# Convolution blocks copied out of their PSUM banks, state-space groups that begin one burst earlier, and two half products ahead of the last group's output

## The chip, the cores and the metric

The kernel runs on one core of a Trainium2 chip. The metric is the device time of the core in microseconds (us), the lower the better. The kernel before takes 2576.32 us, the median of 3 runs (2575.54 to 2577.38).

## The reference

Two layers of a decoder trunk on 512 tokens of width 1024, everything in fp32. Each layer is a SwiGLU feed-forward half-step, a mixer and a second half-step:

```
x <- x + 1/2 * SwiGLU_1(RMSNorm(x))
h  = RMSNorm(x)
[q|k|v|z|xBC|dt|g_sb|g_ssm] = h @ W_in
y_sb  = StickBreakingAttention(q,k,v) @ W_branch_sb     (4 heads x 128)
y_ssm = Mamba2_SSD(z,xBC,dt) @ W_branch_ssm             (24 heads x 64, 8 B/C groups, state 128)
x <- x + (sigmoid(g_sb)*y_sb + sigmoid(g_ssm)*y_ssm) @ W_out
x <- x + 1/2 * SwiGLU_2(RMSNorm(x))
```

`Mamba2_SSD` first sends the xBC columns through a causal depthwise convolution of 4 taps and a SiLU, then runs a scan over four chunks of 128 tokens for each of 8 groups of 3 heads:

```
xbc = silu(causal_depthwise_conv(xbc, conv_w, conv_b)); xs, bm, cm = split(xbc)
cb = C_k B_k^T;  decay = exp(cum_t - cum_s) where s <= t
y_intra = (cb * decay) @ (x * dt);  y_inter = (C @ state) * exp(cum)
new_state = state * exp(cum_end) + (B * to_end)^T @ (x * dt)
y = (y + D * x) * silu(z);  y = y / rms of its group (192 wide) * ssm_norm
```

## The kernel before, in words

**Products.** Every large product is taken in fp32 by three passes of TensorE: weights and activations are split in a high part (`hi`) and a rest (`lo`), and for each block of 128 along the contraction `dense` issues three matmuls at L359, L360 and L361. The weights come block by block through `wraw` (three buffers, DMA issued by SP at L274), are cast to `whi` on ScalarE (L324) and subtracted to `wlo` on VectorE (L326), two units ahead of their use. A unit is the weights of one product (8 blocks; the merge products with `w_branch_ssm` have 12 blocks in two units of 6).

**What sets the order.** The order of each engine's instructions is written out by the program itself: `dense` calls `tick()` after each block of three matmuls, and a tick moves all side tasks (generators set going by `spawn`) one step on; `yield n` waits n ticks. The engines run their rows in that order, each in its own queue, and wait for one another by semaphores. Small matmuls of the side tasks are collected into bursts that stand between two blocks (`gather` sets the tick of the next burst and how many PSUM banks of each pool it may take, `meet` waits for such a place).

**PSUM.** Dense products use four banks `mm`; two banks `pa` and two banks `pt` serve the side tasks. A `mm` bank is reused four products later, once everything that reads it has run.

**The mixer.** After q, k, v and attention, `group_steps` gives an order of projection blocks of 128 columns: b, c and x blocks go to `conv_block`, z blocks to `by_tokens`, which takes all four `mm` banks at once, one for each 128 tokens (384 columns of weights). A pair of groups p = 0 to 3 shares one z block (2 x 192 columns) and three x blocks. `conv_block` reads the product's bank four times: once on ScalarE for the tap without a shift and the bias (L1112), three times on VectorE for the shifted taps (L1115, result `cv` in SBUF). A tanh on ScalarE (L1120) and one more VectorE instruction (L1127) make the SiLU; x and b blocks are then transposed by TensorE (L939) and copied out (L1145, L1154).

**A state-space group** (`ssd_group`, 8 a layer). For each chunk, `prepare` computes `xw` and `xdt` on GpSimd (L1226, L1234), the decays `dec` on ScalarE (L1236, L1238) from cumulative sums `cumb` that SP loads with one buffer (L1190), a mask on GpSimd (L1240) and y = D*x on GpSimd (L1242). `inner` multiplies C by B and the states by TensorE (L1246, L1250), `decay` applies `dec` (L1260), `outer` takes two chunks together (L1268, L1271), adds them to y (L1275 to L1283), multiplies by z (L1287) and sums squares (L1294). When all four chunks are there, GpSimd makes the reciprocal root (L1334, L1335), VectorE and ScalarE apply it (L1343, L1345), TensorE transposes the result (L939) and `y_part` splits it into `yt` (L1364, L1366), the input of the merge products. The next group begins when `ssd_on` becomes False.

**The end of the mixer.** After the last projection come two products of the attention branch (`branch_sb`); `flush` then ticks until all side tasks are done, among them the last group's output; then the merge loop takes for each of 8 column blocks the product of the 12 `yt` blocks with `w_branch_ssm`, in two halves of 6, in the order 6, 7, 0, 1, ... 5. Line numbers move on by 6 at the products and by up to 24 in `ssd_group` with the change.

Of the kernel before, what the change touches and what calls it, by code (L numbers as in the profile page):

```python
# [17 lines left out]
P = 128  # L18
# [9 lines left out]
HPG = 3  # L28
# [26 lines left out]
FRONT = 2  # L55
MERGE_ORDER = tuple(range(EARLY, KB)) + tuple(range(EARLY))
# [67 lines left out]
def unit_order(layer):  # L124

    def ffn(f):
        for s, (j0, j1) in enumerate(slices(layer, f)):
            start = j0
            if s == 0 and not pairs_from(layer, f):
                for key in leading(layer, f):  # L130
                    yield key, KB
                j0 = 4
            for j in range(j0, j1):
                if j < pairs_from(layer, f):
                    yield (layer, f, "gate", j), KB
                    yield (layer, f, "up", j), KB
                elif j % 2 == 0:
                    for part in SEVEN:
                        yield (layer, f, "pair", j, part), KB
            for m in OUT_ORDER:  # L140
                yield (layer, f, "down", s, m), j1 - start

    yield from ffn(1)
    for key in leading(layer, 0):
        yield key, KB
    for t, h in qkv_order():
        yield (layer, t, h), KB
    for kind, i in group_steps():
        if kind == "z":
            for u in range(NT):  # L150
                yield (layer, "z", i, u), 2 * 2 * GW // P + (i == 0)
        else:
            yield (layer, kind, i), KB
    for m in MERGE_ORDER[:2]:
        yield (layer, "bsb", m), SBH
    for i, m in enumerate(MERGE_ORDER):
        yield (layer, "bssm", m, 0), 6
        yield (layer, "bssm", m, 1), 6
        if i + 2 < KB:
            yield (layer, "bsb", MERGE_ORDER[i + 2]), SBH  # L160
    for m in OUT_ORDER:
        yield (layer, "out", m), KB
    yield from ffn(2)
# [12 lines left out]
class Builder:  # L176
# [63 lines left out]
    def meet(self, tag, limit):  # L240

        while self.burst != self.now or not self.free[tag]:
            if limit <= 0 and self.burst <= self.now:
                self.gather(1)
            limit -= 1
            yield 1
        self.free[tag] -= 1

# [855 lines left out]
    def conv_block(self, kind, i, ps):  # L1104
# [7 lines left out]
        nc.scalar.activation(u, ps, AF.Identity, scale=tap[KCONV - 1], bias=tap[KCONV])  # L1112
        yield 2
        for j in range(1, KCONV):
            nc.vector.scalar_tensor_tensor(u[:, j:], ps[:, :SEQ - j], tap[KCONV - 1 - j], u[:, j:],  # L1115
                                           op0=ALU.mult, op1=ALU.add)
            yield 1
# [14 lines left out]
        if kind == "x":  # L1132
            p, i = divmod(i, 3)
            yield from self.meet("pt", (10, 4 + 3 * (p == 0), 10)[i])
# [14 lines left out]
        elif kind == "b":  # L1149
            yield from self.meet("pt", 5)  # L1150
            pt = self.transposed(dst, NT - 1)
            yield 1
            tok = self.t(mp, [P, NT - 1, P], "btok")
            nc.scalar.copy(tok, pt)  # L1154
            self.ssm[i]["btok"] = tok
# [40 lines left out]
    def ssd_group(self, layer, g):  # L1196
# [10 lines left out]
        y = self.t(mp, [P, NT, GW], "y", bufs=1)  # L1207
        ss = self.t(mp, [P, NT], "ss")
        decs, xdts, xws, states, sums = {}, {}, {}, {}, {}
        finished = []  # L1210

        def heads(ap):
            return ap.rearrange("p (h d) -> p h d", d=HD)

        def wide(ap):
            return ap.unsqueeze(2).to_broadcast([P, HPG, HD])
# [11 lines left out]
        def prepare(c):  # L1228
# [13 lines left out]
            nc.gpsimd.tensor_tensor(heads(y[:, c, :]), x, wide(par[:, G_D + h0:G_D + h0 + HPG]), op=ALU.mult)  # L1242
# [19 lines left out]
        def outer(c0):  # L1262
# [10 lines left out]
            yield 2  # L1273
            yc = y[:, c0:c0 + 2, :]
# [28 lines left out]
        self.spawn(prepare(1), 3)  # L1303
        yield 5
# [13 lines left out]
        self.spawn(prepare(3), 5)  # L1318
        yield 8
# [4 lines left out]
        if g < GROUPS - 1:  # L1324
            self.spawn(self.next_cum(g + 1), 1)
        yield 2
        self.gather(1, 2, 0)
        self.spawn(outer(2))
        while len(finished) < NT:
            yield 1  # L1330
        self.give("xs")
        yield 1
        rstd = self.t(mp, [P, NT], "gny")
# [12 lines left out]
        self.ssd_on = False  # L1346
# [6 lines left out]
        for src, blk in todo:  # L1353
            yield from self.meet("pa", 8 if g < GROUPS - 1 else 0)
            pt = self.transposed(src.rearrange("p c d -> p (c d)"), aside=True).rearrange("p c d -> p (c d)")
            self.spawn(self.y_part(pt, blk, par[:, G_SSM + blk:G_SSM + blk + 1]))
# [44 lines left out]
    def mixer(self, layer):  # L1401
# [24 lines left out]
        with ExitStack() as mix:  # L1426
# [18 lines left out]
            with tc.tile_pool(name=f"mp{layer}", bufs=2, reuse_waits="tile") as self.mp:  # L1445
                self.attention_on, self.ssd_on, self.dt_done = False, False, False
                self.groups_left, self.cumb = GROUPS, None
# [25 lines left out]
                for m in MERGE_ORDER[:2]:  # L1473
                    branch_sb(m)
                self.flush()
            with tc.tile_pool(name=f"mg{layer}", bufs=KB, reuse_waits="tile") as mg, \
# [18 lines left out]
                for i, m in enumerate(MERGE_ORDER):  # L1495
                    ps = self.t(self.pmm, [P, SEQ], "mm")
                    self.dense(ps, self.unit(layer, "bssm", m, 0), self.y_ssm, 0, 6, stop=False)
                    self.dense(ps, self.unit(layer, "bssm", m, 1), self.y_ssm, 6, 12, start=False)
                    self.spawn(merge(i, ps))
                    if i + 2 < KB:  # L1500
                        branch_sb(MERGE_ORDER[i + 2])
# [174 lines left out]
```

## Time and profile before

| quantity | value |
|---|---|
| median of 3 runs | 2576.32 us (2575.54 to 2577.38) |
| profiled execution, its own time | 2577.66 us |
| its span in the trace | 2576.0 us, so 1.66 us lie around it |
| mean granted TensorE clock | 0.995 |
| TensorE busy in the span | 2545.2 us, so 30.8 us idle |
| VectorE, ScalarE, GpSimd busy | 1795.5, 1323.5, 551.5 us |

Both layers' state-space stages lie at 560 to 832 us and 1835 to 2108 us of the span. In the profile's rows a name such as `mm<-whi,hhi` reads as output from inputs, PE is TensorE, PEld its weight load, DVE VectorE, ACT ScalarE, POOL GpSimd, SP SyncE; a `q` behind an engine's name is its DMA queue. The clock is told as a share of full speed.

### The profile page before, as it was taken

To read this page: it belongs to the slowest core of one execution; us is meant where nothing else is said; L and a number is where in the kernel's file an instruction comes from. 1 tells how busy PE (TensorE), PEld (TensorE's weight loads), DVE (VectorE), ACT (ScalarE), POOL (GpSimd) and SP (SyncE) were. 2 spreads that over 40 slices of the span, in tenths; PEclk is the share of its full clock that TensorE was granted. 3 is DMA by queue.
4 is the path that set the end of the run, shared out by engine and by line. 5 is a ranking of instruction groups with operands and counts; after the bars stand their busy time and mean duration, and the time that the engine had idled before them with its cause. 6 is when DMAs were issued, how large, how long until landed. Compare 5 with 4: busy or idle time off the path is not lost.

```text
span 2576.0 us, 39402 instructions
## 1 busy us (share of the span) xinstructions
PE 2545.2 (99%) x15536; PEld 2301.7 (89%) x15536; DVE 1795.5 (70%) x2332; ACT 1323.5 (51%) x2181; POOL 551.5 (21%) x656
## 2 busy tenths in 40 slices
PE   9999999999999999999999999999999999999998
PEld 8899998888887889989899999988888878899997
DVE  8586886666765477768896768856666644885766
ACT  6353565665554264435563445656655533653434
POOL 0131300124433001313112222001344320122220
PEclk9999999999999999999999999999999999999999
DMA  4555673232222475656656466622333234756562
GB/s 152 168 140 159 170 203 112 78 114 100 91 91 86 140 209 148 179 152 164 180 126 179 144 174 175 194 80 82 115 99 101 93 94 159 193 140 169 151 164 83
DMA packets 112874, 357.35 MB, mean 139 GB/s; under 512 B 12784, under 2 KB 20400, under 8 KB 112688
## 3 DMA queue, kind: packets, MB, share of 16 engines
q1 hardware_dynamic: 96704, 299.13, 35.1%
q0 software_dynamic: 15120, 55.06, 11.9%
q8 instruction: 122, 2.00, 0.3%
q10 hardware_dynamic: 864, 0.64, 0.1%
q14 instruction: 64, 0.52, 0.1%
HBM read 342.10 MB, written 12.68 MB: 138 GB/s over the span
## 4 chain that ended last, share of the span: by engine, by line
PE 92%; DVE 4%; ACT 2%; issue 1%; POOL 1%; DMA 0%; DVEq 0%; SPq 0%; POOLq 0%; ACTq 0%
PE mm L359 25%; PE mm L361 25%; PE mm L360 25%; PE pa L360 4%; PE pa L359 4%; PE pa L361 4%; PE pa L1268 2%; DVE wlo L326 1%; DVE cv L1115 1%; PE pa L1271 1%; ACT whi L324 1%; PE pt L939 1%; PE pt L1250 1%; PE pt L1246 0%; PE pa L498 0%
## 5 line engine op out<-in xcount | busy, mean ns | idle before, releaser
L324 ACT CAST whi<-wraw 128x1024 fp32r<-128x1024 f32 (+3 forms) x433 | 427.8, 988 | 684.2 <-PE mm L361 436.4
L326 DVE TENSOR_TENSOR wlo<-wraw,whi 128x1024 fp32r<-128x1024 f32 (+3 forms) x433 | 532.7, 1230 | 246.7 <-ACT whi L324 246.0
L359 PE MATMUL mm<-hhi,whi 128*128 128x512 f32 (+1 forms) x1472 | 501.0, 340 | 0.3 <-DVE z L1184 0.3
L361 PE MATMUL mm<-hlo,whi 128*128 128x512 f32 (+1 forms) x1472 | 494.8, 336 | 0.0
L360 PE MATMUL mm<-hhi,wlo 128*128 128x512 f32 (+1 forms) x1472 | 494.3, 336 | 0.0
L361 PEld LDWEIGHTS mm<-hlo,whi 128*128 128x128 f32 x1472 | 276.0, 187 | 30.2
L359 PE MATMUL mm<-th,whi 128*128 128x256 f32 x1080 | 302.2, 280 | 0.8 <-DVE c L648 0.8
L360 PE MATMUL mm<-th,wlo 128*128 128x256 f32 x1080 | 301.6, 279 | 0.2 <-DVE wlo L326 0.2
L359 PEld LDWEIGHTS mm<-hhi,whi 128*128 128x128 f32 x1472 | 276.4, 188 | 28.1 <-DVE z L1184 1.0
L360 PEld LDWEIGHTS mm<-hhi,wlo 128*128 128x128 f32 x1472 | 276.6, 188 | 27.6
L361 PE MATMUL mm<-tl,whi 128*128 128x256 f32 x1080 | 301.3, 279 | 0.0
L326 DVE TENSOR_TENSOR wlo<-s,whi 128x1024 fp32r<-128x1024 f32 x180 | 257.2, 1441 | 35.3 <-ACT whi L324 31.7
L359 PE MATMUL mm<-act,whi 128*128 128x512 f32 (+1 forms) x710 | 273.9, 386 | 0.0
L360 PE MATMUL mm<-act,wlo 128*128 128x512 f32 (+1 forms) x710 | 273.7, 386 | 0.0
L361 PE MATMUL mm<-act,whi 128*128 128x512 f32 (+1 forms) x710 | 273.7, 385 | 0.0
L658 POOL TENSOR_TENSOR g<-g,rs 128x512 f32<-128x512 f32 x70 | 149.3, 2132 | 481.8 <-DVE g L637 452.2
L286 POOL DMA_DIRECT2D s<-in_wflat_dram x105 | 91.9, 900 | 726.4 <-DMA s<-in_wflat_dram 630.6
L324 ACT CAST whi<-s 128x1024 fp32r<-128x1024 f32 x180 | 188.7, 1048 | 61.4 <-PE mm L361 42.2
L359 PEld LDWEIGHTS mm<-th,whi 128*128 128x128 f32 x1080 | 202.7, 188 | 1.0 <-issue 1.0
L361 PEld LDWEIGHTS mm<-tl,whi 128*128 128x128 f32 x1080 | 202.9, 188 | 0.0
L360 PEld LDWEIGHTS mm<-th,wlo 128*128 128x128 f32 x1080 | 202.2, 187 | 0.4 <-DVE wlo L326 0.4
L721 DVE SCALAR_TENSOR_TENSOR x<-mm,x 128x512 f32<-128x512 f32 x93 | 64.2, 690 | 190.2 <-PE mm L361 190.0
(310 smaller groups left out, 5311.0 us busy)
## 6 DMA issues: line engine op xcount, KB each, us to landing
wraw<-in_wflat_dram SPq DMA_DIRECT2D x321, 512.0 KB, 3.6
s<-in_wflat_dram POOLq DMA_DIRECT2D x105, 512.0 KB, 7.5
s<-in_wflat_dram SPq DMA_DIRECT2D x95, 512.0 KB, 5.1
wraw<-in_wflat_dram SPq DMA_DIRECT2D x88, 384.0 KB, 3.1
cumb<-cum_d SPq DMA_DIRECT2D x16, 768.0 KB, 4.5
xd<-x SPq DMA_DIRECT2D x16, 256.0 KB, 5.5
wraw<-in_wflat_dram SPq DMA_DIRECT2D x16, 256.0 KB, 3.4
x<-xd SPq DMA_DIRECT2D x16, 256.0 KB, 5.2
```

The source lines that it names most:

```text
L286: self.nc.gpsimd.dma_start(raw, self.stored(key[:-1] + (part,)), accum_op=ALU.add)
L324: nc.scalar.copy(hi[:, :n], raw[:, :n])
L326: nc.vector.tensor_tensor(lo[:, :n], raw[:, :n], hi[:, :n].bitcast(F32), op=ALU.subtract)
L359: mm(ps, a[0], b[0], start=start, stop=False, **kw)
L360: mm(ps, a[1], b[0], start=False, stop=False, **kw)
L361: mm(ps, a[0], b[1], start=False, stop=stop, **kw)
L658: eng.tensor_tensor(out, r, self.rs[:, cols].unsqueeze(1).to_broadcast([P, 2, SEQ // 2]), op=ALU.mult)
L721: self.nc.vector.scalar_tensor_tensor(x, pd, 0.5, x, op0=ALU.mult, op1=ALU.add)
L939: self.nc.tensor.transpose(pt[:, cs], src[:, cs], self.ident)
L1115: nc.vector.scalar_tensor_tensor(u[:, j:], ps[:, :SEQ - j], tap[KCONV - 1 - j], u[:, j:], op0=ALU.mult, op1=ALU.add)
L1250: nc.tensor.matmul(pu, btok[:, c, :], xws[c].rearrange("p h d -> p (h d)"), start=True, stop=True)
L1268: nc.tensor.matmul(near[:, at:at + HD], decs[c][:, i, :], xdts[c][:, i, :], start=True, stop=True)
```

## The change

**Convolution.** ScalarE first copies the bank to the SBUF tile `raw` (which later takes the tanh); the activation and the three VectorE instructions then read that copy. A bank is free when the copy is done.

**State-space groups.** `ssd_on` becomes False one tick behind the second `outer` and no longer behind the normalisation. y = D*x moves out of `prepare` into a task `direct` of two chunks each, which takes the one y tile when the group before has normalised its own (`y_busy`); `outer` waits for it. The load of the next group's `cumb` is set going some ticks earlier. The transposes of y may use a `pa` or a `pt` bank and look for a place for up to 16 ticks, no longer 8.

**Merge.** With AHEAD = 2, the first halves of products 6 and 7 (blocks 0 to 5 of `yt`, 18 matmuls each) stand ahead of `flush`, so ahead of the last group's transposes; the order of the weight units follows.

```diff
+AHEAD = 2
@@ units
+    for m in MERGE_ORDER[:AHEAD]:
+        yield (layer, "bssm", m, 0), 6
     for i, m in enumerate(MERGE_ORDER):
-        yield (layer, "bssm", m, 0), 6
+        if i >= AHEAD:
+            yield (layer, "bssm", m, 0), 6
         yield (layer, "bssm", m, 1), 6
@@ Builder
-    def meet(self, tag, limit):
-
-        while self.burst != self.now or not self.free[tag]:
+    def meet(self, limit, *tags):
+
+        while self.burst != self.now or not any(self.free[tag] for tag in tags):
...
+        tag = next(tag for tag in tags if self.free[tag])
         self.free[tag] -= 1
+        return tag
@@ conv_block
-        nc.scalar.activation(u, ps, AF.Identity, scale=tap[KCONV - 1], bias=tap[KCONV])
+        nc.scalar.copy(r, ps)
+        nc.scalar.activation(u, r, AF.Identity, scale=tap[KCONV - 1], bias=tap[KCONV])
         yield 2
         for j in range(1, KCONV):
-            nc.vector.scalar_tensor_tensor(u[:, j:], ps[:, :SEQ - j], tap[KCONV - 1 - j], u[:, j:],
+            nc.vector.scalar_tensor_tensor(u[:, j:], r[:, :SEQ - j], tap[KCONV - 1 - j], u[:, j:],
@@ ssd_group
-        y = self.t(mp, [P, NT, GW], "y", bufs=1)
-            nc.gpsimd.tensor_tensor(heads(y[:, c, :]), x, wide(par[:, G_D + h0:G_D + h0 + HPG]), op=ALU.mult)
+        def direct(c0):
+            while self.y_busy not in (None, g):
+                yield 1
+            if self.y_busy is None:
+                self.y_busy = g
+                begun.append(self.t(mp, [P, NT, GW], "y", bufs=1))
+            for c in (c0, c0 + 1):
+                nc.gpsimd.tensor_tensor(heads(begun[0][:, c, :]), heads(xs[:, c, :]),
+                                        wide(par[:, G_D + h0:G_D + h0 + HPG]), op=ALU.mult)
+            begun.append(c0)
...
+            while c0 not in begun:
+                yield 1
...
         self.spawn(prepare(0))
         self.spawn(prepare(1), 3)
+        self.spawn(direct(0), 6)
...
         self.spawn(prepare(3), 5)
+        self.spawn(direct(2), 7)
+        if g < GROUPS - 1:
+            self.spawn(self.next_cum(g + 1), 7)
...
-        if g < GROUPS - 1:
-            self.spawn(self.next_cum(g + 1), 1)
         yield 2
         self.gather(1, 2, 0)
         self.spawn(outer(2))
+        yield 1
+        self.ssd_on = False
...
-        self.ssd_on = False
+        self.y_busy = None
...
-            yield from self.meet("pa", 8 if g < GROUPS - 1 else 0)
+            tag = yield from self.meet(16 if g < GROUPS - 1 else 0, "pa", "pt")
@@ mixer
+                def first_half(m):
+                    sums[m] = self.t(self.pmm, [P, SEQ], "mm")
+                    self.dense(sums[m], self.unit(layer, "bssm", m, 0), self.y_ssm, 0, 6, stop=False)
+
+                for m in MERGE_ORDER[:AHEAD]:
+                    first_half(m)
                 self.flush()
...
-                    ps = self.t(self.pmm, [P, SEQ], "mm")
-                    self.dense(ps, self.unit(layer, "bssm", m, 0), self.y_ssm, 0, 6, stop=False)
-                    self.dense(ps, self.unit(layer, "bssm", m, 1), self.y_ssm, 6, 12, start=False)
+                    if i >= AHEAD:
+                        first_half(m)
+                    self.dense(sums[m], self.unit(layer, "bssm", m, 1), self.y_ssm, 6, 12, start=False)
```

**The end of the mixer on TensorE, layer 0.** The rows begin with the last block of the attention branch's second product (`ohi`); `pa<-ident` are the transposes of the last group's output, `yt` the blocks of earlier groups. Before:

```order
L359 MATMUL mm_8058<-ohi_5356,whi_7967 128x512
L360 MATMUL mm_8058<-ohi_5356,wlo_7968 128x512
L361 MATMUL mm_8058<-olo_5357,whi_7967 128x512
L939 MATMUL pa_8108<-ident,raw_8102 128x128 x4
L939 MATMUL pa_8113<-ident,acc_7830 128x128 x4
L359 MATMUL mm_8141<-yt_5914,whi_8043 128x512
L360 MATMUL mm_8141<-yt_5914,wlo_8044 128x512
```

Now the attention product is followed by

```order
L367 MATMUL mm_8086<-olo_5360,whi_7995 128x512
L365 MATMUL mm_8122<-yt_6047,whi_8071 128x512
L366 MATMUL mm_8122<-yt_6047,wlo_8072 128x512
L367 MATMUL mm_8122<-yt_6048,whi_8071 128x512
L365 MATMUL mm_8122<-yt_6269,whi_8071 128x512
```

and the transposes stand further on:

```order
L365 MATMUL mm_8155<-yt_6923,whi_8092 128x512
L366 MATMUL mm_8155<-yt_6923,wlo_8093 128x512
L367 MATMUL mm_8155<-yt_6924,whi_8092 128x512
L945 MATMUL pa_8186<-ident,raw_8167 128x128 x4
L945 MATMUL pa_8191<-ident,acc_7854 128x128 x4
L365 MATMUL mm_8122<-yt_7265,whi_8128 128x512
L366 MATMUL mm_8122<-yt_7265,wlo_8129 128x512
```

The two transposes stood right behind the attention product and stand now behind 36 matmuls more, 18 of `mm_8122` and 18 of `mm_8155`; what follows them is the second half of `mm_8122`.

**ScalarE around the z block of pair p = 1, layer 0.** In the rows of before `mm_5806` is the bank of the x block just ahead of that z block, whose four banks are `mm_5897`, `mm_5917`, `mm_5927`, `mm_5939`. Before:

```order
L1120 ACTIVATE raw_5819<-cv_5820 128x512
L324 CAST whi_5901<-wraw_5754 128x768
L1112 ACTIVATE cv_5908<-mm_5806,conv_4679 128x512
L1364 ACTIVATE yt_5914<-pa_5883,par_109 128x512
L324 CAST whi_5951<-wraw_5807 128x768
L1120 ACTIVATE raw_5907<-cv_5908 128x512
L1145 ACTIVATE xs_5982<-pt_5959 128x4x128
```

Now the x block's bank is `mm_5848`, and the z block's are `mm_5938`, `mm_5961`, `mm_5977`, `mm_5987`:

```order
L330 CAST whi_5942<-wraw_5772 128x768
L1242 ACTIVATE dec_5946<-cumb_5715,sq_4941 128x128 x3
L1244 ACTIVATE dec_5946<-dec_5946 128x384
L1118 COPY raw_5953<-mm_5848 128x512
L1119 ACTIVATE cv_5954<-raw_5953,conv_4679 128x512
L1313 ACTIVATE t_963_5966,ss_5745<-y_5872 128x192 x2
L330 CAST whi_6000<-wraw_5849 128x768
```

Further on, where before a cast `whi_6075` stood right ahead of the first z bank's reader, there now stands

```order
L330 CAST whi_6110<-wraw_5995 128x1024
L1242 ACTIVATE dec_6113<-cumb_5971,sq_4941 128x128 x3
L1244 ACTIVATE dec_6113<-dec_6113 128x384
L1369 ACTIVATE acc_5865<-y_5872,gny_6092 128x64 x4
L1242 ACTIVATE dec_6136<-cumb_5971,sq_4941 128x128 x3
L1244 ACTIVATE dec_6136<-dec_6136 128x384
L1189 ACTIVATE z_6145<-mm_5938 128x384
L1189 ACTIVATE z_6155<-mm_5961 128x384
```

Between the cast `whi_5942` and the first reader of the x block's bank there are now four instructions of group 1's decays (`dec_5946`), and that reader is a copy; ahead of the first z bank's reader there are the decays of two chunks of the next group and the tail of group 1 (`acc_5865`).

**GpSimd at the same place.** The `xw` and `xdt` of group 1 (from `xs_5517` before, `xs_5523` now) feed its first burst of inner products. Before:

```order
L1287 TENSOR_TENSOR y_5524<-y_5524,z_4931 128x192
L1334 TENSOR_SCALAR ss_5525<-ss_5525 128x4
L1335 TENSOR_TENSOR gny_5797<-ss_5525,small 128x4
L1226 TENSOR_TENSOR xw_5842<-xs_5517,sq_4941 128x192
L1234 TENSOR_TENSOR xdt_5844<-xs_5517,sq_4941 128x192
L1240 AFFINE_SELECT dec_5841<-dec_5841 128x384
L1242 TENSOR_TENSOR y_5832<-xs_5517,par_109 128x192
L1226 TENSOR_TENSOR xw_5861<-xs_5517,sq_4941 128x192
L1234 TENSOR_TENSOR xdt_5863<-xs_5517,sq_4941 128x192
L1240 AFFINE_SELECT dec_5860<-dec_5860 128x384
L1242 TENSOR_TENSOR y_5832<-xs_5517,par_109 128x192
```

Now:

```order
L1232 TENSOR_TENSOR xw_5763<-xs_5523,sq_4941 128x192
L1240 TENSOR_TENSOR xdt_5765<-xs_5523,sq_4941 128x192
L1246 AFFINE_SELECT dec_5762<-dec_5762 128x384
L1302 TENSOR_TENSOR y_5586<-y_5586,t_922_5781 128x384
L1306 TENSOR_TENSOR y_5586<-y_5586,z_4911 128x192
L1232 TENSOR_TENSOR xw_5795<-xs_5523,sq_4941 128x192
L1240 TENSOR_TENSOR xdt_5797<-xs_5523,sq_4941 128x192
L1306 TENSOR_TENSOR y_5586<-y_5586,z_4931 128x192
L1246 AFFINE_SELECT dec_5794<-dec_5794 128x384
L1358 TENSOR_SCALAR ss_5530<-ss_5530 128x4
L1359 TENSOR_TENSOR gny_5838<-ss_5530,small 128x4
L1256 TENSOR_TENSOR y_5872<-xs_5523,par_109 128x192 x2
```

Before, group 1 began behind the reciprocal root of group 0 (`gny_5797`), and its y = D*x (`y_5832`) stood within its own preparation. Now its first `xw`, `xdt` and mask stand ahead of the last additions to group 0's y, its second `xw` behind one of these and one product with z, and its y = D*x (`y_5872`) behind the root of group 0 (`gny_5838`).

More of the change, by code (lines that the diff above doesn't have):

```diff
@@ L1133, in conv_block @@
             p, i = divmod(i, 3)
-            yield from self.meet("pt", (10, 4 + 3 * (p == 0), 10)[i])
+            yield from self.meet((10, 4 + 3 * (p == 0), 10)[i], "pt")
             pt = self.transposed(dst)
@@ L1149, in conv_block @@
         elif kind == "b":
-            yield from self.meet("pt", 5)
+            yield from self.meet(5, "pt")
             pt = self.transposed(dst, NT - 1)
@@ L1206, in ssd_group @@
         cumb = self.cumb
-        y = self.t(mp, [P, NT, GW], "y", bufs=1)
         ss = self.t(mp, [P, NT], "ss")
         decs, xdts, xws, states, sums = {}, {}, {}, {}, {}
-        finished = []
+        finished, begun = [], []
         def heads(ap):
@@ L1273, in outer @@
             yield 2
+            while c0 not in begun:
+                yield 1
+            y = begun[0]
             yc = y[:, c0:c0 + 2, :]
@@ L1332, in ssd_group @@
         yield 1
+        y = begun[0]
         rstd = self.t(mp, [P, NT], "gny")
@@ L1353, in ssd_group @@
         for src, blk in todo:
-            yield from self.meet("pa", 8 if g < GROUPS - 1 else 0)
-            pt = self.transposed(src.rearrange("p c d -> p (c d)"), aside=True).rearrange("p c d -> p (c d)")
+            tag = yield from self.meet(16 if g < GROUPS - 1 else 0, "pa", "pt")
+            pt = self.transposed(src.rearrange("p c d -> p (c d)"), aside=tag == "pa").rearrange("p c d -> p (c d)")
             self.spawn(self.y_part(pt, blk, par[:, G_SSM + blk:G_SSM + blk + 1]))
@@ L1446, in mixer @@
                 self.attention_on, self.ssd_on, self.dt_done = False, False, False
-                self.groups_left, self.cumb = GROUPS, None
+                self.groups_left, self.cumb, self.y_busy = GROUPS, None, None
                 self.room = {"raw": self.ROOM, "cv": self.ROOM, "xs": 3, "z": NT}
@@ L1474, in mixer @@
                     branch_sb(m)
+                sums = {}
+                def first_half(m):
[3 more added lines that the diff above has]
+                    first_half(m)
                 self.flush()
@@ L1495, in mixer @@
                 for i, m in enumerate(MERGE_ORDER):
-                    ps = self.t(self.pmm, [P, SEQ], "mm")
-                    self.dense(ps, self.unit(layer, "bssm", m, 0), self.y_ssm, 0, 6, stop=False)
-                    self.dense(ps, self.unit(layer, "bssm", m, 1), self.y_ssm, 6, 12, start=False)
-                    self.spawn(merge(i, ps))
+                    if i >= AHEAD:
+                        first_half(m)
+                    self.dense(sums[m], self.unit(layer, "bssm", m, 1), self.y_ssm, 6, 12, start=False)
+                    self.spawn(merge(i, sums.pop(m)))
                     if i + 2 < KB:
```

## The prediction

> **What bounds the kernel now.** I read the page's busy shares and its chain first, then TensorE's waits, then windows around them, last the timeline inside these.
>
> ```profile
> PE 2545.2 (99%) x15536; PEld 2301.7 (89%) x15536; DVE 1795.5 (70%) x2332; ACT 1323.5 (51%) x2181; POOL 551.5 (21%) x656
> PE 92%; DVE 4%; ACT 2%; issue 1%; POOL 1%; DMA 0%; DVEq 0%; SPq 0%; POOLq 0%; ACTq 0%
> ```
>
> TensorE (PE) is busy 99% of the span and carries 92% of the chain. The change leaves PE the same number of rows, so it can win only PE's idle time and what the clock loses behind it. TensorE's waits over the whole run:
>
> ```profile
> PE mm L359 <- DVE cv L1115: 11.1, 6, 2.7
> PE pa L939 <- DVE raw L1343: 7.5, 2, 3.7
> ...
> PE pt L1250 <- POOL xw L1226: 0.2, 1, 0.2
> ```
>
> (Total us, times, longest.) Two causes make 18.6 of 30.8 us: a product waits for a bank that a convolution still reads, six times, and the last group's transposes wait for its normalisation, twice. The windows (length, busy PE, PEld, DVE, ACT, POOL, then granted clock) show where, and at what clock:
>
> ```profile
> 588.00:604.00 16.00, 13.31 (x78) 12.80 (x77) 9.44 (x17) 7.22 (x15) 3.54 (x7) 0.89 0.19 67
> 664.00:680.00 16.00, 15.13 (x102) 14.77 (x101) 10.67 (x19) 9.47 (x22) 5.02 (x9) 1.00 0.40 133
> 736.00:752.00 16.00, 14.01 (x76) 13.44 (x75) 7.40 (x13) 5.50 (x13) 7.33 (x11) 0.89 0.33 115
> 816.00:832.00 16.00, 12.27 (x52) 9.99 (x51) 4.96 (x8) 4.69 (x12) 3.37 (x5) 0.89 0.36 115
> 1863.00:1879.00 16.00, 13.32 (x86) 12.74 (x85) 9.55 (x17) 8.45 (x18) 4.87 (x10) 1.00 0.24 81
> 2011.00:2027.00 16.00, 14.02 (x78) 13.62 (x77) 6.84 (x12) 5.60 (x12) 6.93 (x11) 0.89 0.37 116
> 2090.00:2106.00 16.00, 12.27 (x47) 9.93 (x46) 5.25 (x9) 4.69 (x12) 3.37 (x5) 0.79 0.35 108
> 560.00:830.00 270.00, 260.55 (x1394) 231.00 (x1393) 173.33 (x274) 150.54 (x348) 110.11 (x175) 0.98 0.28 94
> ```
>
> Each layer has four stalls. The timeline of layer 0 names them (idle before the row in brackets):
>
> ```profile
> 595.81 0.41 PE L359 MATMUL mm<-whi,hhi 128*128 128x384 f32 x1 [2.69 <-DVE cv L1115]
> ...
> 670.30 0.41 PE L359 MATMUL mm<-whi,hhi 128*128 128x384 f32 x1 [0.87 <-DVE cv L1115]
> ...
> 742.23 0.41 PE L359 MATMUL mm<-whi,hhi 128*128 128x384 f32 x1 [1.99 <-DVE cv L1115]
> ...
> 821.64 0.69 PE L939 MATMUL pa<-ident,raw 128*128 128x128 f32 x4 [3.73 <-DVE raw L1343]
> ```
>
> The first three are the fourth bank of the z blocks of pairs 1, 2, 3. Behind a stall the clock may halve. A clock of 0.89 over 16 us is 16 x 0.11 = 1.8 us lost, 0.79 is 3.4. Behind the 0.87 us stall nothing is lost, behind 1.99 us 1.8 in both layers, behind 2.69 us 1.8 in layer 0 and nothing in layer 1, behind 3.73 us 1.8 and 3.4.
>
> **Part 1, what goes: the end of the mixer.** 2 x 3.73 = 7.5 us of idling and 5.1 of clock (1.76 + 3.36), together 12.6. Cover: two half products of 18 matmuls. Their pace is
>
> ```profile
> 816.16 0.39 PE L361 MATMUL mm<-olo,whi 128*128 128x512 f32 x1
> ...
> 817.52 0.39 PE L361 MATMUL mm<-olo,whi 128*128 128x512 f32 x1
> ...
> 820.80 0.69 DVE L1343 TENSOR_TENSOR raw<-y,gny 128x512 f32<-128x512 f32 x1 [2.17 <-POOL gny L1335]
> ...
> 823.09 1.60 DVE L1366 SCALAR_TENSOR_TENSOR yt<-pa,par,yt 128x512 fp32r<-128x512 f32 x2 [1.60 <-ACT yt L1364]
> ```
>
> six in 1.36 us, 0.227 each, so 36 take 8.2 us. The attention product ends near 817.9; the transposes would be reached at 826.1, and what they wait for is done at 821.5: 4.6 us to spare. Late next: the half product behind them reads blocks 6 to 9 first (12 matmuls, 2.7 us), then the last group's. Before, the split was done 3.05 us after the transposes' start (824.69 - 821.64), its first half 0.8 earlier; PE wants them 1.2 + 2.7 = 3.9 us after that start. So nothing waits: 0.
>
> **Part 2, what goes: the z blocks' bank.** 11.1 us of idling and 3 x 1.8 = 5.3 of clock, together 16.4, if the bank is free in time. Today it is read by an activation and three VectorE instructions behind other work; in future by one copy. The copy's size is that of another bank copy, and the queue ahead of it on ScalarE is made of these:
>
> ```profile
> L1373 ACT COPY gs<-mm x2: 568/568/568, 504.8 to 1780.5; 128x512 f32<-128x512 f32 x2
> ...
> L1112 ACT ACTIVATE cv<-mm,conv 128x512 f32<-128x512 f32 x21 | 16.2, 771 | 0.0
> ...
> L324 ACT CAST whi<-wraw 128x768 fp32r<-128x768 f32 x15 | 12.4, 828 | 18.6 <-PE mm L360 11.1 <-issue 4.1 <-PE mm L361 3.3
> ...
> 601.59 0.99 ACT L1236 ACTIVATE dec<-cumb,sq 128x128 f32<-128x128 f32 x3 [0.94 <-PE pa L1268]
> ...
> 603.04 0.97 ACT L1236 ACTIVATE dec<-cumb,sq 128x128 f32<-128x128 f32 x3
> ```
>
> The fourth bank is wanted 18 matmuls into the z block:
>
> ```profile
> 589.68 0.47 PE L359 MATMUL mm<-whi,hhi 128*128 128x384 f32 x1
> ...
> 592.78 0.34 PE L361 MATMUL mm<-wlo,hhi 128*128 128x384 f32 x1
> ```
>
> 3.1 us from the first start to the last, 0.175 a matmul, so 3.2 after the block's start. For pairs 2 and 3 the order puts a cast and the copy ahead: 0.83 + 0.57 = 1.4, at most 2.2 with one activation (0.77) more; both stalls go. For pair 1 the cast, one chunk of decays (1.45 from one chunk's start to the next) and the copy come to 2.85, 3.1 to 3.4 with the waits between them: I take 0.2 us left, with ends 0 and 1.0 (another activation of 0.77 ahead).
>
> **Part 3, what the earlier groups add.** The order moves the first burst of groups 1 to 6 ahead by 35, 44, 27, 24, 9 and 6 rows; group 7's stays. No stall of before is named there, so I give it no gain. Its prices, per layer, all at pair 1, where two groups now overlap:
> - First z bank, wanted by the product behind the z block. ScalarE has ahead of it, from the end of the z block's third unit: a cast of 1024 columns, a chunk of decays, the tail, a second chunk, then tanh, and VectorE one more reader.
>
> ```profile
> L324 ACT CAST whi<-wraw 128x1024 fp32r<-128x1024 f32 x23 | 24.1, 1048 | 25.4 <-PE mm L360 14.0 <-PE mm L361 11.4
> ...
> L1182 ACT ACTIVATE z<-mm 128x384 f32<-128x384 f32 x12 | 5.7, 485 | 4.3 <-PE mm L361 3.3 <-POOL y L1287 1.0
> ...
> 820.80 1.06 ACT L1345 ACTIVATE acc<-y,gny 128x64 f32<-128x64 f32 x4 [1.42 <-POOL gny L1335]
> ...
> L1184 DVE SCALAR_TENSOR_TENSOR z<-z,mm 128x384 f32<-128x384 f32 x12 | 6.5, 550 | 6.7 <-ACT z L1182 6.7
> ```
>
>   1.05 + 1.45 + 1.06 + 1.45 + 0.49 + 0.55 = 6.05, against the fourth unit's 24 x 0.175 = 4.2 and a few small matmuls: 1.3, ends 0 and 1.9.
> - The first burst's second `xw` stands behind an addition and a product of the group before on GpSimd, which come behind ScalarE and VectorE work of the convolutions: 0.7, ends 0 (today's 0.2 for all such waits) and 2.0 (the addition in full, 1.02 by the next row, an instruction of 0.51 and a clash of 0.45, both below).
>
> ```profile
> 816.66 1.02 POOL L1283 TENSOR_TENSOR y<-y,t 128x384 f32<-128x384 f32 x1 [4.68 <-DVE t L1279]
> ```
>
> - Transposes behind a decay product that stands behind a `wlo` and three taps on VectorE, and smaller margins: 0.9 together, ends 0 and 2.2 (three taps of 0.745, below).
>
> With the 0.2 of part 2 that is 3.1 us a layer, ends 0 and 7.1. Each is under 1.9 us, so I allow one slow clock stretch in the run, 1.8 us. The Trainium skill, "TensorE: Matmul & The Clock Gate", Part 1, has the clock halve after an idle window of about 3.4 us; the trace shows it behind 1.99 us. By that rule the allowance would be 0 and the time 1.8 us less.
>
> **Part 4, at nothing.** 28 copies a layer add 28 x 0.57 = 16 us to ScalarE's 150.5 in the stage of 270 us: 62% at most. The VectorE taps read two SBUF tiles:
>
> ```profile
> L1115 DVE SCALAR_TENSOR_TENSOR cv<-mm,conv,cv 128x510 f32<-128x510 f32 x22 | 16.4, 746 | 0.6
> ...
> 598.35 0.69 DVE L1127 SCALAR_TENSOR_TENSOR cv<-raw,cv 128x512 f32<-128x512 f32 x1 [2.68 <-ACT raw L1120]
> ...
> 582.27 0.97 DVE L1127 SCALAR_TENSOR_TENSOR cT<-raw,cv 128x512 f32<-128x512 f32 x1 [0.76 <-ACT raw L1120]
> ...
> 582.66 0.96 POOL L1234 TENSOR_TENSOR xdt<-xs,sq 128x192 f32<-128x192 f32 x1
> ...
> 588.47 0.51 POOL L1234 TENSOR_TENSOR xdt<-xs,sq 128x192 f32<-128x192 f32 x1
> ```
>
> 0.69 when alone, 0.97 beside a GpSimd instruction, which itself then takes 0.96 in place of 0.51. Over 84 taps a layer VectorE goes from -5 to +19 us on 173: hidden by its idle 97. On SP the `cumb` loads stand ahead of up to two weight loads, so these wait with them.
>
> ```profile
> SPq L1190 <- ACT dec L1236: 18.2, 6, 6.6
> ...
> POOL xdt L1234 <- PE pa L1268: 56.6, 8, 10.7
> ```
>
> The wait for the last decays is 6.6 us at the longest; behind it are weight casts that wait in this stage for PE (25.4 and 18.6 us above), for no DMA. Were that cover gone, a load would come up to 6.6 us late.
>
> **Sum.** -12.6 - 16.4 + 2 x 3.1 + 1.8 = -21.0 us. The profiled run, 2577.66 (span 2576.0 and 1.66 around), lies 1.34 over the median, so 2577.66 - 21.0 - 1.34 = 2555.3.
>
> **The rivals.**
> - *Waits in another place* (0.22). The order on ScalarE puts the copy behind more work than I count, or the new waits take their upper ends; of the gains only the end is sure, since 4.6 us of cover stand against it. 2576.3 - 12.6 = 2563.7, with 6.2 of new waits 2569.9. For it: both engines run in order and two groups now share them. Against: pairs 2 and 3 have 1.0 us to spare or more.
> - *A shared port holds GpSimd up* (slower, 0.08). Each tap that meets a GpSimd instruction costs that one 0.45 us (0.96 - 0.51), and GpSimd's `xw` and `xdt` release PE's bursts, two a group, 32 in both layers. At two clashes a burst without slack, 32 x 0.9 = 28.8: 2555.3 + 28.8 = 2584.1. It decides the sign from 0.66 us a burst on (21 / 32). Against it: GpSimd itself waits 56.6 us a stage for PE (last fence), 7 a group, and PE waited for `xw` only 0.2 us. The Trainium skill, "SBUF — State Buffer", section "Who interferes with whom", says that a VectorE instruction with two SBUF inputs contends with a GpSimd instruction that reads SBUF, one with a single SBUF input doesn't; the rows above agree, and by it the change turns all 168 taps from the harmless form to the other.
> - *It does less than it says* (0.10): the z stalls and the end go, but decays, tails and copies make as many waits as went, within 0.2% of before (5.2 us, about what a measurement can tell), so near 2576. For it: ScalarE's extra 16 us lie in the very stretches where PE waited. Against: PE's end has none of them.
> - My forecast: 0.60, on its own 2546 to 2562 (all new waits 0: 2576.3 - 29.0 = 2547.3).
>
> The range takes in the first rival with its new waits: 2546 to 2570. Faster by over 0.2% (below 2571.2): 0.60 + 0.22 = 0.82; within: 0.10; slower (over 2581.5): 0.08.
>
> **What would show it.** In the changed profile: PE's wait for `raw` at the transposes gone and the clock 1.00 behind the mixer's end (part 1); no wait of a 384-column matmul for a convolution at pairs 2 and 3, under 0.5 us at pair 1 (part 2); small waits for `xw`, `dec` or `z` around pair 1, some 3 us a layer (part 3); taps between 0.69 and 0.97 and GpSimd slower beside them (part 4). Wrong would be a wait over 1.9 us at a burst, a second half product that waits for `yt`, or a weight cast that waits for DMA.

## The result, and the profile after

The changed kernel takes 2563.82 us (median of 6 runs, 2560.5 to 2565.36) against 2576.64 us before (6 runs): a ratio of 0.995, 95% interval 0.9937 to 0.9963. The forecast was 2555, range 2546 to 2570. The time lies in the range, 8.8 us above the forecast and at the figure of the first rival, 2563.7; whether for that rival's reason is what the experiments are for. It lies 1.8 us above the upper end that the forecast had on its own (2546 to 2562): it is in the range because the range took in that rival.

The profiled execution took 2560.5 us (span 2558.5), 3.3 under the median. Its page has this row:

```profile
PE 2536.8 (99%) x15536; PEld 2291.7 (90%) x15536; DVE 1810.5 (71%) x2332; ACT 1355.0 (53%) x2237; POOL 578.0 (23%) x656
```

TensorE's idle time fell from 30.8 us to 2558.5 - 2536.8 = 21.7. ScalarE gained 31.5 us of work, VectorE 15.0, GpSimd 26.5, although GpSimd has no instruction more. TensorE's waits (total us, times, longest):

```profile
PE pt L1266 <- POOL xw L1232: 3.7, 2, 1.8
PE pt L945 <- DVE dec L1276: 3.5, 4, 1.1
PE pt L945 <- ACT btok L1161: 1.7, 2, 0.9
...
PE mm L365 <- DVE z L1191: 1.0, 2, 0.5
```

Both old causes are gone, the convolution's hold on the banks and the wait of the last transposes. New are four small waits a layer, and the wait for `z` grew from 0.3 to 1.0 us; these rows come to 9.9 us. (`btok` is the copy of a transposed b block out of its bank, `bT` the b block ahead of its transposition, `acc` a part of the last step of a group's normalisation, which ScalarE does.) The timeline of layer 0:

```profile
551.39 1.16 PE L945 MATMUL pt<-ident,cv 128*128 128x128 f32 x8 [0.86 <-ACT btok L1161]
565.25 0.52 PE L945 MATMUL pt<-ident,bT 128*128 128x128 f32 x3 [0.64 <-DVE dec L1276]
592.07 0.59 PE L1266 MATMUL pt<-xw,btok 128*128 128x192 f32 x2 [1.84 <-POOL xw L1232]
603.97 0.63 PE L945 MATMUL pt<-ident,cv 128*128 128x128 f32 x4 [1.15 <-DVE dec L1276]
```

The windows (same columns as before) at the ends of the two mixers and at the longest new wait:

```profile
812.00:830.00 18.00, 18.00 (x90) 15.24 (x90) 8.42 (x13) 5.74 (x14) 3.46 (x5) 1.00 0.47 150
2079.00:2097.00 18.00, 18.00 (x91) 15.24 (x90) 8.42 (x13) 5.74 (x14) 3.46 (x5) 1.00 0.48 152
584.00:600.00 16.00, 14.16 (x79) 12.54 (x78) 10.42 (x19) 9.84 (x23) 10.05 (x15) 1.00 0.16 59
```

The mixers' ends have no idle time left and the clock is at 1.00. In this execution the clock didn't halve behind the 1.84 us wait either; its mean clock is 0.999, that of the five other runs 0.998 or 0.997. No trace of those five was kept.

### The profile page after: what moved, and what is told of

Its sections match the earlier page's. It is cut to its first block, busy times and chain, and to the rows that moved or that the text cites. A ratio compares the mean times of both kernels' runs of the same rounds, so it can differ in the third digit from the quotient of the medians.

```text
span 2558.5 us, 39470 instructions
## 1 busy us (share of the span) xinstructions
PE 2536.8 (99%) x15536; PEld 2291.7 (90%) x15536; DVE 1810.5 (71%) x2332; ACT 1355.0 (53%) x2237; POOL 578.0 (23%) x656
## 4 chain that ended last, share of the span: by engine, by line
PE 91%; DVE 4%; ACT 3%; POOL 1%; issue 1%; DMA 0%; SPq 0%; DVEq 0%; ACTq 0%; POOLq 0%
PE mm L365 25%; PE mm L366 24%; PE mm L367 24%; PE pa L366 4%; PE pa L365 4%; PE pa L367 4%; PE pa L1284 2%; DVE cv L1122 1%; ACT whi L330 1%; DVE wlo L332 1%; PE pa L1287 1%; PE pt L945 1%; PE pt L1266 0%; PE pt L1262 0%; ACT cv L1119 0%
```

## The experiments

Times stand beside the kernel before on the same chip: 2576.88 us for the first four runs, 2576.84 for the next four, 2576.57 for the last. With 2576.64 beside the whole change, these agree within 0.4 us, so runs of different chips are compared below. Two theories went in. Theory 1 is the prediction's: the copies take the waits at the banks away, the halves those at the end, and the groups' earlier begin brings the new small waits. Theory 2: the copies bring these, through ScalarE and the taps. The first four runs take the change's three parts apart.

**The copies alone.** The kernel before, with this edit alone:

```diff
-        nc.scalar.activation(u, ps, AF.Identity, scale=tap[KCONV - 1], bias=tap[KCONV])
+        nc.scalar.copy(r, ps)
+        nc.scalar.activation(u, r, AF.Identity, scale=tap[KCONV - 1], bias=tap[KCONV])
...
-            nc.vector.scalar_tensor_tensor(u[:, j:], ps[:, :SEQ - j], tap[KCONV - 1 - j], u[:, j:],
+            nc.vector.scalar_tensor_tensor(u[:, j:], r[:, :SEQ - j], tap[KCONV - 1 - j], u[:, j:],
```

> The copies of the convolution alone, on the kernel before. Theory 1 (each part does one thing: the copies remove the z banks' waits, the groups' earlier begin adds the new small waits): 11.1 us of waits and 5.3 us of clock go, nothing comes, 2576.6 - 16.4 = 2560.2. Theory 2 (the copies themselves bring the new waits, through 31 us more on ScalarE and slower GpSimd instructions beside the taps): the z waits go but some 5 us a layer of other waits stand in the trace, about 2570. In both the transposes at the end still wait 3.7 us per layer for the normalisation.

Measured: 2576.13 us (11 runs), ratio 0.9999 (0.999 to 1.0008): no change. TensorE's waits:

```profile
PE pa L939 <- DVE raw L1344: 7.5, 2, 3.7
PE pt L1251 <- POOL xw L1227: 2.5, 4, 0.8
PE pt L939 <- DVE bT L1128: 2.5, 2, 1.3
PE pt L939 <- DVE dec L1261: 1.8, 4, 0.5
PE pt L939 <- ACT btok L1155: 1.7, 2, 0.9
PE pt L939 <- DVE cv L1128: 1.3, 2, 0.7
PE pt L1247 <- DVE dec L1261: 1.2, 2, 0.6
PE pt L1247 <- ACT btok L1155: 1.1, 2, 0.6
...
PE pa L1269 <- DVE dec L1261: 0.9, 2, 0.5
```

The 11.1 us at the z blocks' banks are gone, as both theories had it, and 13.0 us of small waits stand in their place (13.5 is what the later expectation calls them), with the groups where they were. TensorE's idle time in the profiled execution is 31.9 us against 30.8; its mean clock is 0.998 against 0.995, and its busy time 3.1 us less. So the new waits cost a little more than the old ones, and the clock gives that back. Theory 1, which put the small waits down to the groups' earlier begin, falls; what theory 2 says of the copies holds, with a larger price than it named (2570). Which part of the copies makes the waits isn't shown yet.

**The groups' earlier begin alone.** All of the change in `ssd_group`, `meet` and `next_cum`, without the copies and the halves:

```diff
+        self.spawn(direct(0), 6)
...
+        yield 1
+        self.ssd_on = False
...
-        self.ssd_on = False
+        self.y_busy = None
```

> The earlier begin of the state-space groups alone, on the kernel before (with the wider choice of banks for the transposes). Theory 1: no stall goes, and the new waits for xw, dec and banks come, up to 5 us a layer: 2577 to 2587. Theory 2 (the earlier begin is what takes the z banks' waits away, or is harmless without the copies): 2576.6 or less, and no wait for xw over 0.5 us.

Measured: 2568.88 us (8 runs, 2566.04 to 2572.33), ratio 0.9971 (0.9961 to 0.9982). A gain of 8.0 us, where theory 1 had a loss. The waits:

```profile
PE pa L941 <- DVE raw L1362: 7.5, 2, 3.7
PE mm L361 <- DVE cv L1117: 5.3, 2, 2.7
...
PE mm L361 <- DVE z L1186: 1.0, 2, 0.5
```

Four of the six waits at the z blocks' fourth bank are gone, those of pairs 2 and 3, and no wait for `xw` has come; the waits for `z` and `wlo` grew by 1.0 us together. Why shows in the timeline at pair 3 of layer 0, TensorE's rows, then one of VectorE:

```profile
740.99 0.34 PE L363 MATMUL mm<-wlo,hhi 128*128 128x384 f32 x1
741.16 0.60 PE L941 MATMUL pt<-ident,cv 128*128 128x128 f32 x4
741.60 1.45 PE L1279 MATMUL pa<-xdt,dec 128*128 128x64 f32 x12
742.89 0.87 PE L1282 MATMUL pa<-state,cT 128*128 128x192 f32 x4
743.80 0.41 PE L361 MATMUL mm<-whi,hhi 128*128 128x384 f32 x1
...
741.35 2.31 DVE L1117 SCALAR_TENSOR_TENSOR cv<-mm,conv,cv 128x511 f32<-128x511 f32 x3
```

The fourth bank would be wanted at 741.16, and the taps that read it run till 743.66. With the groups ahead, a burst of transposes and outer products lies in just that gap (741.16 to 743.8). Before, the same place was an idle 1.99 us, and such a burst came behind it. The bank isn't free earlier: the taps end 5.6 us after the z block's start (738.02), before 5.2 (742.08 against 736.93). Other work is at hand. At pair 2 such a burst fills the place in the same way (671.48 to 674.12).

**The two half products alone.**

```diff
+                for m in MERGE_ORDER[:AHEAD]:
+                    first_half(m)
                 self.flush()
```

> The two half products ahead of the last output alone, on the kernel before. Both theories: 2 x 3.73 us of idling and 5.1 us of clock behind it go, 2576.6 - 12.6 = 2564.0; the z banks' waits of 2.7, 0.9 and 2.0 us a layer stay. Above 2568 the halves would bring a wait of their own, which the trace would show behind the transposes.

Measured: 2564.38 us (5 runs), ratio 0.9953 (0.9941 to 0.9966). 12.5 us gained, 12.6 expected, and the wait for `raw` is gone from the list; the banks' 11.1 us are there as before:

```profile
PE mm L363 <- DVE cv L1119: 11.1, 6, 2.7
```

So one part of the three brings all that the whole change brings.

**Copies and halves, without the groups.** The edits of the first and the third experiment together.

> The copies and the two half products, without the groups' earlier begin. Theory 1: all stalls of before go and none of the new ones comes, 2576.6 - 16.4 - 12.6 = 2547.6, faster than the whole change (2563.8). Theory 2: the new waits stay with the copies, 2560 to 2566, no better than the whole change.

Measured: 2565.3 us (5 runs), ratio 0.9957 (0.9945 to 0.997): theory 2's figure, 0.9 us above the halves alone. The copies bring nothing here either.

**Groups and halves, without the copies.** The second and the third together; the convolution is that of before.

> The whole change without the convolution's copies. Theory 3 (formed on the four runs before: the groups' earlier begin takes the waits of pairs 2 and 3 away and adds almost none, the copies bring the small waits): the gains of the two parts add up, 2576.9 - 8.0 - 12.5 = 2556.4, faster than the whole change by 7; left in the trace is the z block of pair 1, 2.7 us a layer. Rival (the copies are needed once groups overlap and the halves stand ahead): 2563.8 or more, as the whole change.

Measured: 2558.25 us (2558.06 to 2558.49), ratio 0.9927 (0.9915 to 0.994): 5.6 us under the whole change. The parts' gains, 8.0 and 12.5, come to 18.6 together, not 20.5. The 1.9 us are less than the interval of the 8.0 alone (some 2.7 us to either side). In the profiled executions the idle time adds up nearly (5.0 and 7.6 us gained, 12.0 together); TensorE's busy time, in which the clock shows, doesn't (4.3 and 5.7 us less, 7.4 together). One place of that can be seen: behind the stall of pair 1 the clock is 0.89 over 16 us in both layers here (from 590 and from 1858 us), with the groups alone 0.91 over 20 us in layer 0 (from 586) and 1.00 in layer 1 (1866 to 1882). What is left of the old waits is

```profile
PE mm L365 <- DVE cv L1121: 5.3, 2, 2.7
```

the z block of pair 1, where no burst lies in the gap.

**One copy a layer.** The kernel of the last run, and a copy in one of the 28 blocks, the x block ahead of that z block:

```diff
+        if (kind, i) == ("x", 4):
+            nc.scalar.copy(r, ps)
+            ps = r
         nc.scalar.activation(u, ps, AF.Identity, scale=tap[KCONV - 1], bias=tap[KCONV])
```

> The kernel of groups_ahead with one copy a layer: only the x block just ahead of the z block of pair 1 is copied out of its bank. Theory 3: the last 2.7 us a layer go, and some 2 us of clock behind them, 2556.4 - 5.4 - 2 = 2549, with no wait for xw, btok or dec over 0.5 us. Rival (a copy at that very place makes ScalarE and the taps late for the burst behind it): the stall is replaced by waits of 1 to 2 us, 2553 to 2557.

Measured: 2552.21 us (4 runs, 2552.09 to 2552.82), ratio 0.9904 (0.9891 to 0.9918), the fastest kernel of this study: 24.6 us under before and 11.6 under the whole change. The time lies between the two theories' figures. The stall of 2.7 us is replaced by one of 1.1, as the rival had it and theory 3 had ruled out (none over 0.5): in layer 0, transposes wait for a decay product that VectorE computes behind two taps of the copied block. 2549 was missed by 3.2 us, of which 1.9 had been missed already by the kernel that this one starts from (2558.25 for 2556.4); the new waits (2.1 us for `dec` in both layers) are more than the rest:

```profile
PE pt L945 <- DVE dec L1278: 2.1, 2, 1.1
...
PE mm L365 <- DVE z L1193: 1.0, 2, 0.5
```

**What makes the copies dear.** They add work to ScalarE, and they turn the taps into instructions with two SBUF inputs. This run has the first and not the second:

```diff
 (conv_only)
-            nc.vector.scalar_tensor_tensor(u[:, j:], r[:, :SEQ - j], tap[KCONV - 1 - j], u[:, j:],
+            nc.vector.scalar_tensor_tensor(u[:, j:], ps[:, :SEQ - j], tap[KCONV - 1 - j], u[:, j:],
```

> conv_only with the copy and the activation from it kept, but the three VectorE taps reading the PSUM bank again, so with one SBUF input each. ScalarE has the same work as in conv_only; VectorE and GpSimd no longer meet at two SBUF inputs. If ScalarE's longer queue makes the small waits of conv_only (13.5 us in the run, for xw, bT, dec, btok and cv), 10 us or more of them stay, beside the z banks' 11 us, which come back: 2583 or more. If the taps' second SBUF input makes them, under 3 us of them stay, and the time is that of before with its z waits some 0.6 us longer each, 2577 to 2581, GpSimd's product with z at 0.60 to 0.70 us as before (0.65).

Measured: 2586.12 us (5 runs), ratio 1.0036 (1.0023 to 1.0049), slower than before. The waits:

```profile
PE mm L359 <- DVE cv L1116: 12.7, 6, 3.4
...
PE pt L939 <- ACT btok L1155: 1.4, 2, 0.7
PE pt L1251 <- POOL xw L1227: 1.3, 2, 0.7
PE pt L1247 <- ACT btok L1155: 1.1, 2, 0.6
...
PE pt L1247 <- DVE dec L1261: 1.0, 2, 0.5
...
PE pt L939 <- DVE dec L1261: 0.4, 2, 0.2
```

The time is in the range of the first cause (2583 or more). But 5.2 us of small waits stay of 13.0, which is neither cause's figure (10 or more; under 3), so both seem to count. GpSimd's product with z is back at 632 ns a piece in the stage of layer 0, where conv_only had 770 and before 650. How much of the rest the long waits at the banks (12.7 us, they are back) merely cover can't be read here. The next run is without that blur.

**The same on the whole change.** All copies stay; the taps read the bank, but in the one block where the copy frees a bank that is waited for:

```diff
 (the whole change)
-            nc.vector.scalar_tensor_tensor(u[:, j:], r[:, :SEQ - j], tap[KCONV - 1 - j], u[:, j:],
+            nc.vector.scalar_tensor_tensor(u[:, j:], (r if (kind, i) == ("x", 4) else ps)[:, :SEQ - j], tap[KCONV - 1 - j], u[:, j:],
```

> The whole change with all 28 copies a layer and the activations that read them, but the VectorE taps read the copy only in the x block ahead of the z block of pair 1, and the PSUM bank in the other 27. ScalarE has the work of the whole change, while 81 of 84 taps a layer have one SBUF input again. If ScalarE's longer queue makes the small waits, those of the whole change (xw 3.7, dec 3.5, btok 1.7, z 1.0 us) stay, 2562 to 2565. If the taps' second SBUF input makes them, the waits for xw go below 1 us and the time comes to that of one_copy, 2552 to 2555. A middle, as taps_from_bank had it (5.2 of 13.5 us stayed), would be 2557 to 2560. The z banks of pairs 2 and 3 may come back, since these taps begin 0.6 us later than in one_copy; then the trace shows waits for cv there.

Measured: 2556.56 us (2556.24 to 2557.11), ratio 0.9925 (0.9911 to 0.9938): between the two causes' figures, just under the middle's 2557 to 2560. No wait for a convolution at the z banks has come back; the waits for `xw` are 1.6 us, for `dec` 2.6, for `btok` 1.5. The way from one_copy to the whole change is thereby cut in two: 27 more copies on ScalarE, with the activations that read them, cost 2556.56 - 2552.21 = 4.35 us, the second SBUF input of 27 blocks' taps 2563.82 - 2556.56 = 7.26 us. Of the 7.26, 3.94 lie between the two profiled executions (2560.5 and 2556.56); the other 3.3 are what the whole change's median lies above its profiled execution, at the lower clock. GpSimd shows the second part. Its product with z, grouped by form over the stage of layer 0, first of before, then of the whole change, then of this run (count, total us, mean ns):

```profile
L1287 POOL TENSOR_TENSOR y<-y,z 128x192 f32<-128x192 f32 x32 | 20.5, 650 | 0.6
```

```profile
L1306 POOL TENSOR_TENSOR y<-y,z 128x192 f32<-128x192 f32 x32 | 27.5, 868 | 0.6
```

```profile
L1306 POOL TENSOR_TENSOR y<-y,z 128x192 f32<-128x192 f32 x32 | 20.8, 660 | 0.6
```

and in the timeline the instructions ahead of the longest new wait with the taps beside them, of the whole change and of this run:

```profile
589.07 2.57 DVE L1122 SCALAR_TENSOR_TENSOR cv<-raw,conv,cv 128x511 f32<-128x511 f32 x3
...
589.58 1.52 POOL L1256 TENSOR_TENSOR y<-xs,par 128x192 f32<-128x192 f32 x2 [2.09 <-ACT acc L1369]
...
591.06 0.95 POOL L1232 TENSOR_TENSOR xw<-xs,sq 128x192 f32<-128x192 f32 x1
```

```profile
588.68 0.97 POOL L1256 TENSOR_TENSOR y<-xs,par 128x192 f32<-128x192 f32 x2 [2.88 <-ACT acc L1369]
...
588.77 1.53 DVE L1122 SCALAR_TENSOR_TENSOR cv<-mm,conv,cv 128x510 f32<-128x510 f32 x2
...
589.61 0.51 POOL L1232 TENSOR_TENSOR xw<-xs,sq 128x192 f32<-128x192 f32 x1
...
590.18 0.59 PE L1266 MATMUL pt<-xw,btok 128*128 128x192 f32 x2 [0.78 <-POOL xw L1232]
```

The same three instructions take 2.47 us beside taps from SBUF and 1.48 beside taps from the bank. The wait for `xw` falls with it from 1.84 to 0.78 us. VectorE pays as well: its taps from the bank take 734 to 751 ns here, those from SBUF in the whole change 733 to 1132, and its busy time is 1794.8 us against 1810.5. How much of the 7.26 comes through each engine isn't taken apart.

**The longest new wait.** The rows above also say whom that `xw` stands behind: two products y = D*x, which wait for the tail of the group before on ScalarE (`acc`). In this run they come later:

```diff
 (the whole change)
-        self.spawn(direct(0), 6)
+        self.spawn(direct(0), 12)
```

> The whole change with y = D*x of the first two chunks set going at 12 ticks and not at 6, so that GpSimd computes the third chunk's xw before the two products that wait for the tail of the group before. If those products are what holds the first burst up, PE's waits for xw (3.7 us in the run) go: 2563.8 - 3.7 = 2560, or lower if clock was lost behind them. Rival (xw is late for another reason, as the taps that slow GpSimd): the waits for xw stay over 2 us and the time within 1.5 us of 2563.8.

Measured: 2558.74 us (5 runs, 2557.87 to 2559.76), ratio 0.993 (0.9916 to 0.9943). TensorE's waits for `xw` are gone from the list:

```profile
PE pt L945 <- DVE dec L1276: 3.4, 4, 1.1
```

By the medians 5.1 us are gained for 3.7 us of waits. Between the profiled executions it is 1.9 us (2560.5 to 2558.63), since new waits for `c` and `wlo` take 1.0 back and TensorE's busy time is 1.2 longer. The other 3.2 us go with the clock: all five runs have a mean of 0.999, where those of the whole change had 0.998 or 0.997 but for the profiled one. That this clock was lost behind the 1.84 us wait is argued and not shown, for want of a trace of those executions. For it speaks that taps_bank_but_one, where that wait is 0.78 us, has 0.999 in all five runs too.

So the wait for `xw` has two causes that work together, the slower GpSimd instructions and their order. Another order takes all of it away, faster instructions 2.1 of the 3.7 us. So the 5.1 us here and the 7.26 of the run before are in part the same microseconds; no run has both edits. Groups and halves without copies have the order of the whole change and taps from the bank, and no wait for `xw` at all.

## Why the prediction was right or wrong

**Part 1, the end of the mixer: right.** 12.6 us forecast, 12.5 measured with the halves alone; the second half product that follows the transposes doesn't wait.

**Part 2, the z blocks' bank: right on what goes, wrong on who takes it away.** In the whole change no z block waits for a convolution, pair 1 included (0.2 us were allowed there). But pairs 2 and 3 needed no copy: the groups' burst fills their gap. The copy was needed at one block of 28 a layer.

**Part 3, the price of the overlap: named the wrong cause, and too small in all.** It gave the earlier groups no gain; they gain 8.0 us by themselves. It put the new waits on them; groups without copies show 1.0 us for `z` (0.3 before) and half a microsecond for a `wlo`. The whole change shows 9.9 us, 6.2 were forecast. Place by place: 1.3 us for the first z bank were 0.5; 0.7 us for `xw` were 1.84, inside the ends of 0 and 2.0 but at another instruction than the one named, the third `xw` of the group behind the y = D*x pair; 0.9 us for "transposes behind a decay product and smaller margins" were 0.86 + 0.64 + 1.15 = 2.65. The clock allowance of 1.8 us wasn't spent in the profiled execution, and more than spent in the others, whose median lies 3.4 above it.

**Part 4, "at nothing": the step that failed.** It reckoned engine by engine with totals: ScalarE at 62% and VectorE with 97 us to spare a stage. The extra work came out as reckoned (31.5 us on ScalarE for 2 x 16; 15.0 on VectorE between the ends of -10 and +38; a tap took 733 to 1132 ns, for the 0.69 to 0.97 us named). But these engines run their rows in order, and what they have to spare isn't at the places where a burst waits for them. There it cost 4.35 us through ScalarE and 7.26 through the taps' second SBUF input, 11.6 against one copy a layer. One copy a layer, which has next to none of this work, takes 2552.2 us, 3.1 under the forecast, with 3.1 us of new waits (2.1 for `dec`, 1.0 for `z`) where the sum has 6.2. The price of part 3 was thus too high for the groups, and part 4's zero too low for the copies; the two errors cancel in part, and that the miss is no larger is luck.

**The sum.** The forecast takes 21.0 us off the profiled execution, 2577.66 to 2556.7. The profiled execution after took 2560.5, 3.8 us more, and the new waits of 9.9 us where the sum has 6.2 are nearly all of that. TensorE's busy time fell by 8.4 us, where the clock's terms in the sum come to 5.1 + 5.3 - 1.8 = 8.6. The other 4.7 of the 8.5 us between 2555.3 and the median are no mechanism of the sum: it put the median 1.34 us under the profiled execution, and it came out 3.3 above.

**The rivals.** "Waits in another place" gave the measured time, 2563.7, but not by its mechanism: the copy is early enough at every z block, and the bank waits do go. Its second condition, new waits at their upper ends (2 x 7.1 us), was met in part, 9.9, and by waits that come with the copies. "It does less than it says" missed the time, but its reason, ScalarE's extra work in the stretches where TensorE waited, is what the copies alone show: 13.0 us of new waits for 11.1 of old. The slower rival, GpSimd held up by a shared port, names a mechanism that the runs bear out; at 7.3 us over the run, VectorE's share included, it doesn't reach the 21 us from which it would have decided the sign. The Trainium skill, "SBUF — State Buffer", section "Who interferes with whom", states the condition (two SBUF inputs on VectorE), and the trace agrees: 868 ns against 650 with the input moved, 660 with it moved back.

## What to carry to other kernels

A copy that frees a bank early pays only at the product that would wait for this bank: find that one, and leave the other blocks alone (one copy a layer was worth 6.0 us, 27 more cost 4.35 and their readers 7.26; a later place for two GpSimd products won 5.1 us back as well). A stall on a resource can be filled as well as removed: other work ordered into the gap took four of six such waits away, for 1.0 us of new ones. An engine's free time over a stage says nothing on work added in front of an instruction that the critical engine waits for; look at the queue ahead of that instruction.

## What was not expected of the hardware

ScalarE's activation became slower, not faster, when its input moved from the bank to SBUF. By source line, the kernel before and the whole change (min/median/max ns):

```profile
L1112 ACT ACTIVATE cv<-mm,conv x56: 759/772/796, 495.9 to 2059.6; 128x512 f32<-128x512 f32 x56
```

```profile
L1119 ACT ACTIVATE cv<-raw,conv x56: 813/816/821, 496.5 to 2050.6; 128x512 f32<-128x512 f32 x56
```

44 ns more. The Trainium skill, "Perfetto Trace Analysis", section "Optimizing Scalar/DVE Operations", gives ScalarE an access overhead of about 93 ns on SBUF and 51 on PSUM; the difference of 42 agrees. The section calls these engine-busy times and has the profiled latency at about twice that; the rows here differ by the figure itself and not by twice it.

The clock differs from execution to execution of one kernel: the whole change ran at 2560.5 us with a mean clock of 0.999, and at 2563.5 to 2565.4 with 0.998 or 0.997. With the 1.84 us wait removed, five runs lay within 1.9 us of each other, at 0.999. Stalls of one length differ too: behind the 2.7 us stall of pair 1 the clock over 16 us was 0.89 in layer 0 and 1.00 in layer 1 of before, and 0.89 in both layers of the groups and halves without copies.
